# Differential attention in a two-layer diffusion backbone: values after two units in the program, three sets of turned halves, maps combined on VectorE, 16 of 18 key tiles turned by DMA

## The chip, the cores and the metric

The kernel runs on one core of a Trainium2 chip. Its time is the device time of one execution, in microseconds (us). Three executions of the kernel before took 4000.66, 4001.03 and 4004.86 us, so the median is 4001.03 us. In the text PE is TensorE, DVE is VectorE, ACT is ScalarE, POOL is GpSimd and SP is SyncE, whose queue issues all the DMAs spoken of here.

## The reference, cut to what matters

Two layers run over 2048 latent tokens and a prefix of 256 context tokens. The stage that the change touches is the differential attention of the second layer: four heads, each with two softmax maps over all 2304 keys, whose difference weighs the values.

```python
def diff_attend(q, k, v, lam):
    sc = jnp.einsum('bqhmd,bkhmd->bhmqk', q, k).astype(jnp.float32) * SCALE
    p = jax.nn.softmax(sc, axis=-1)
    a = (p[:, :, 0] - lam * p[:, :, 1]).astype(v.dtype)
    return jnp.einsum('bhqk,bkhe->bqhe', a, v)
```

Its output is normalised per head, gated, multiplied by the output projection, added to the residual stream and normalised once more. All of this runs in the same stage.

## The kernel before

The program is written with a tile framework: pools of buffers (a pool's `bufs` is how many copies of a tile exist), and a scheduler that orders the instructions of each engine by the written order, by priorities and by its own estimate of when each is ready. Each engine then works through its list strictly in that order. So an instruction that waits holds up everything behind it on its engine.

The stage starts at `c_pools` in `layer1` and covers the last 1240 us or so of the program. It works on 64 **units**: a unit is one head (of four) and one tile of 128 queries (of sixteen). Heads 0 and 1 come one after the other; heads 2 and 3 alternate in pairs of tiles. For each unit:

- `c_map` is called for map 1, then for map 0. PE multiplies the queries with the keys, which are kept as a high and a low half (`KH`, `KL`, float16). The scores go into two tiles in PSUM: `pSa` (1024 columns, 4 matmuls) and `pSb` (1280 columns, 6 matmuls). There is one copy of each, so the scores of the next map wait until the exponential has read those of this one. DVE takes the maxima (`mx`: one reduction over `pSa`, two over `pSb`), joins them (`cm`), makes the bias (`cnb`), and ACT writes the exponentials to `E1` or `E0` (two instructions, L1419), with their sums.
- From the sums DVE computes `rho`, the factor of map 1 against map 0.
- `c_halves` combines the two maps into `E1` (rho times map 1 plus map 0) and turns them so that keys lie on the partitions. Of the 18 key tiles, the first `DMAK` = 12 are combined on DVE in two instructions of 768 columns (L1432); the last 6 on POOL in two passes (L1429, L1430). The DMA part is cast to float16 on ACT (`H`), the remainder is subtracted on POOL (`L`), and `H` and `L` are each turned by two DMA transposes into `HT` and `LT`, issued from SP. The other 6 tiles are turned on PE into `pTr` (four, then two) and split into halves by ACT (`HT`) and DVE (`LT`).
- `c_values` multiplies the turned halves with the values: 3 matmuls for each of 18 key tiles, 54 in all, into `pO`. `finish` normalises and stores the result.

The loop in `layer1` writes the values one unit behind: the first half of the values of unit n-1 stands after map 1 of unit n, the second half after map 0, held in `pend`. `HT`, `LT`, `H`, `L` and `E1` have two copies, `E0` one. Between these steps `fill` lets a `Filler` put pieces of the output projection (`out_pair`: `yT`, `pX`, `ot`, `xo`) in at a fixed rate; `part` multiplies `ya` by the gate `gl` for it.

## Time and profile before

| | |
|---|---|
| median of three executions | 4001.03 us |
| the profiled execution's own time | 4010.3 us |
| its span in the profile | 4008.2 us |
| the stage, first `rho` to the end of the span | 2775.6 to 4008.2 us |
| PE, DVE, ACT, POOL busy over the whole span | 86%, 69%, 58%, 58% |

The page is one execution on the chip. Matmuls are pipelined, so PE counts as busy longer than it works; to see how fast PE works, take the distance between the starts of two matmuls, not the duration of one. A row of a timeline ends with the idle time of its engine before it and what ended that, in square brackets. The granted clock of TensorE has two levels in the rows, 1.00 (2.4 GHz) and 0.50 (1.2 GHz); a number between them is a mean over a stretch.

### The profile page before, as it was taken

Reading aid. Unit: us, or ns where it says so; the run is one execution under the profiler, and the core shown is the slowest. Engines: PE = TensorE matmul, PEld = TensorE weight load, DVE = VectorE, ACT = ScalarE, POOL = GpSimd, SP = SyncE. Lnnn points to the kernel's source line nnn. Section 1 sums busy time; section 2 is a strip of 40 time slices with the busy share of each in tenths; the row PEclk is TensorE's granted clock in tenths of the full one; section 3 lists DMA queues with packets and bytes.
Section 4 is the critical chain, followed back from the end, with each engine's and each line's share of the span. In section 5 each row is a group of like instructions: output and inputs, shape, how many; then the busy total and the mean of one; then the engine's idle time right before and its main releaser. Section 6 shows DMA issues by size and latency. Waiting matters only on the chain. (4 is left out here: it accounts for less than half of the span.)

```text
span 4008.2 us, 94016 instructions
## 1 busy us (share of the span) xinstructions
PE 3442.4 (86%) x37378; PEld 2679.9 (67%) x37378; DVE 2757.8 (69%) x6515; ACT 2334.3 (58%) x4294; POOL 2304.9 (58%) x2015
## 2 busy tenths in 40 slices
PE   7879989899989999999899999996677677677666
PEld 5659978789867777777688899984444444344443
DVE  5647788996576766665769986754666656666666
ACT  5215546556688877787636566664455444545554
POOL 3204466764388888887635553432565655666655
PEclk9989999999999999999999999998788888778888
DMA  7875433343521111110454442227344434233343
GB/s 235 209 188 121 109 79 97 82 100 89 151 88 47 57 47 47 48 58 27 152 118 94 99 117 73 67 78 206 90 98 117 98 86 116 63 91 96 88 91 83
DMA packets 657711, 400.69 MB, mean 100 GB/s; under 512 B 412342, under 2 KB 608246, under 8 KB 656758
## 3 DMA queue, kind: packets, MB, share of 16 engines
q1 hardware_dynamic: 657270, 394.68, 38.0%
q8 instruction: 292, 4.78, 0.5%
q14 instruction: 149, 1.22, 0.1%
HBM read 207.69 MB, written 106.90 MB: 78 GB/s over the span
## 5 line engine op out<-in xcount | busy, mean ns | idle before, releaser
L80 PE MATMUL pmm<-wk,hT 128*128 128x256 f16 x10848 | 1363.8, 276 | 63.1 <-DVE HL L365 18.8
L80 PEld LDWEIGHTS <-hT 128*128 128x128 f16 x10848 | 1035.4, 99 | 202.9 <-issue 47.5
L781 POOL TENSOR_TENSOR L<-Pm,H 128x1024 f16<-128x1024 f32 (+1 forms) x320 | 617.9, 1954 | 133.4 <-ACT H L779 82.9
L512 POOL TENSOR_TENSOR Pl<-Sb,Ph 128x640 f16<-128x640 f32 (+4 forms) x288 | 438.8, 1524 | 420.3 <-ACT Ph L511 253.2
L750 DVE TENSOR_REDUCE mx<-pM 128x1 f32<-128x512 f32 (+1 forms) x640 | 393.6, 634 | 218.8 <-PE pM L80 212.6
L80 PE MATMUL pO<-V,HT 128*128 128x128 f16 x2304 | 266.6, 239 | 196.4 <-DMA HT<-H 195.0
L80 PE MATMUL pX<-wo,yT 128*128 128x512 f16 x1554 | 400.9, 384 | 38.6 <-DVE yT L891 29.6
L776 ACT ACTIVATE Pm<-pS,esc_a 128x1024 f32<-128x1024 f32 (+1 forms) x320 | 324.5, 1027 | 150.6 <-PE pS L80 102.3
L80 PEld LDWEIGHTS <-Q 128*128 128x128 f16 x2072 | 218.0, 108 | 274.7 <-issue 191.1
L80 PEld LDWEIGHTS <-HT 128*128 128x128 f16 x2304 | 201.4, 108 | 239.2 <-DMA HT<-H 220.2
L80 PE MATMUL pO<-V,H 128*128 128x65 f16 (+1 forms) x4608 | 305.6, 193 | 1.4 <-DVE ya L1260 1.1
L779 ACT CAST H<-Pm 128x1024 f16<-128x1024 f32 (+1 forms) x320 | 302.2, 960 | 6.2 <-PE pO L80 0.3
L80 PEld LDWEIGHTS <-H 128*128 128x128 f16 x4608 | 264.9, 98 | 52.2 <-DVE ya L1260 2.8
L80 PEld LDWEIGHTS <-KL 65*128 65x128 f16 x2672 | 261.5, 98 | 52.2 <-issue 23.5
L80 PE MATMUL pO<-V,L 128*128 128x65 f16 x2304 | 277.4, 196 | 4.0 <-POOL L L781 3.6
L80 PE MATMUL pS<-Qt,KH 128*128 128x256 f16 x1152 | 279.5, 273 | 0.3 <-ACT Pm L776 0.3
L80 PE MATMUL pS<-Q,KL 65*128 65x256 f16 x1152 | 275.6, 274 | 0.0
L912 POOL TENSOR_TENSOR xo<-xo,ot 128x512 f32<-128x512 f32 x105 | 136.2, 1297 | 237.1 <-DVE ot L911 227.1
L80 PEld LDWEIGHTS <-yT 128*128 128x128 f16 x1632 | 155.1, 98 | 172.1 <-issue 36.9
L80 PE MATMUL pO<-V,LT 128*128 128x128 f16 x1152 | 238.4, 239 | 31.0 <-DMA LT<-L 20.5
L1419 ACT ACTIVATE E<-pSa,cnb,esc_c 128x1024 f32<-128x1024 f32 x128 | 154.0, 1203 | 160.5 <-DVE cnb L1415 155.1
L511 ACT CAST Ph<-Sb 128x640 f16<-128x640 f32 (+4 forms) x288 | 219.5, 762 | 47.9 <-PE pO L80 42.3
(327 smaller groups left out, 8569.4 us busy)
## 6 DMA issues: line engine op xcount, KB each, us to landing
qk<-qkst SPq DMA_DIRECT2D x104, 256.0 KB, 2.4
wmod<-w_mod SPq DMA_DIRECT2D x24, 1024.0 KB, 8.1
xo<-x SPq DMA_DIRECT2D x48, 512.0 KB, 3.8
xt<-x SPq DMA_DIRECT2D x34, 512.0 KB, 4.7
G<-zz SPq DMA_DIRECT2D x68, 256.0 KB, 2.4
x<-xo SPq DMA_DIRECT2D x34, 512.0 KB, 3.1
wst<-w_in_even SPq DMA_DIRECT2D x13, 1024.0 KB, 5.6
wst<-w_in_odd SPq DMA_DIRECT2D x13, 1024.0 KB, 5.7
```

The costliest lines, as they stand in the source:

```text
L80: return self.nc.tensor.matmul(out=out, lhsT=l, rhs=r, start=s, stop=e, skip_group_check=skip)
L511: nc.scalar.copy(out=H[:, :n * P], in_=Sb[:, :n * P])
L512: nc.gpsimd.tensor_tensor(out=L[:, :n * P], in0=Sb[:, :n * P], in1=H[:, :n * P], op=ALU.subtract)
L750: nc.vector.tensor_reduce(out=mx[:, j:j + 1], in_=ps[:, :n], op=ALU.max, axis=AX.X)
L776: nc.scalar.activation(out=Pm[:, :n], in_=S[:, :n], func=AF.Exp, scale=esc[0], bias=LNP)
L779: nc.scalar.copy(out=H[:, :n], in_=Pm[:, :n])
L781: eng.tensor_tensor(out=L[:, :n], in0=Pm[:, :n], in1=H[:, :n], op=ALU.subtract)
L912: (nc.vector if l and self.late else nc.gpsimd).tensor_tensor(out=xo[:, cs], in0=xo[:, cs], in1=tt, op=ALU.add)
L1419: nc.scalar.activation(out=E[:, c0:c0 + w], in_=S[i][:, :w], func=AF.Exp, scale=esc[0], bias=nb, accum_out=ss[:, i:i + 1])
```

## The change

All edits lie in the stage of differential attention.

- **Values two units behind.** `pend` becomes a list, and the loop writes the values of a unit only when two units are pending, so two steps after its maps; at the end the last two units' values follow one another. `HT` and `LT` get three copies.
- **Combining on DVE alone.** POOL's two passes are gone. DVE runs three instructions over columns 0 to 1024, 1024 to 2048 and 2048 to 2304.
- **16 of 18 key tiles turned by DMA.** `DMAK` is 16: `H`, `L` and each transpose are 1024 columns instead of 768, four transposes a unit as before. PE turns 2 tiles instead of 6.
- **Priority.** Both `c_map` calls of every unit are moved ahead by 80 in the scheduler's priority (`boostC`); before, only the first unit's map 1 was (by 1000).
- **Room.** The rotary tables get a pool of their own that is closed before the stage, and the gate tiles `gl` have one copy instead of two. The load of a head's values is written before the maps of its first unit, not after them.

```diff
-    DMAK = 12
+    DMAK = 16
+    boostC = 80
...
-        self.gp = self.pool(s, "gC", 2)
+        self.gp = self.pool(s, "gC", 1)
...
-        HT = self.wp.tile([P, NT, P], F16, name="HT")
-        LT = self.wp.tile([P, NT, P], F16, name="LT")
-        nc.gpsimd.tensor_scalar(out=E1[:, nd:], in0=E1[:, nd:], scalar1=rho, scalar2=None, op0=ALU.mult)
-        nc.gpsimd.tensor_tensor(out=E1[:, nd:], in0=E1[:, nd:], in1=E0[:, nd:], op=ALU.add)
-        for c0, c1 in ((0, nd // 2), (nd // 2, nd)):
+        HT = self.wp.tile([P, NT, P], F16, name="HT", bufs=3)
+        LT = self.wp.tile([P, NT, P], F16, name="LT", bufs=3)
+        for c0, c1 in ((0, nd // 2), (nd // 2, nd), (nd, NTOK)):
             nc.vector.scalar_tensor_tensor(out=E1[:, c0:c1], in0=E1[:, c0:c1], scalar=rho, in1=E0[:, c0:c1],
                                            op0=ALU.mult, op1=ALU.add)
...
+            self.rs.close()
             wo, kv = self.c_pools(s)
...
+            pend = []
+
+            def values(half):
+                if half == 0:
+                    self.Oc = self.pO.tile([P, 512], F32, name="pO")[:, 0:P]
+                u, halves, V, s0 = pend[0]
+                self.c_values(self.Oc, *halves, V, range(9) if half == 0 else range(9, NT))
+                if half:
+                    pend.pop(0)
+                    finish(u, self.Oc, s0)
...
-                with first:
+                with self.tc.high_priority(offset=self.early if n == 0 else self.boostC):
                     E1, s1 = self.c_map(u, 1, Qs[1, h, qt // 2][:, q], ks[1], escs[h // 2], shift[1])
-                if pend:
-                    O = self.pO.tile([P, 512], F32, name="pO")[:, 0:P]
-                    self.c_values(O, *pend[1], pend[2], range(0, 9))
+                if len(pend) == 2:
+                    values(0)
...
-                E0, s0 = self.c_map(u, 0, Qs[0, h, qt // 2][:, q], ks[0], escs[h // 2], shift[0])
+                with self.tc.high_priority(offset=self.boostC):
+                    E0, s0 = self.c_map(u, 0, Qs[0, h, qt // 2][:, q], ks[0], escs[h // 2], shift[0])
...
-                if pend:
-                    self.c_values(O, *pend[1], pend[2], range(9, NT))
-                    finish(pend[0], O, pend[3])
...
+                if len(pend) == 2:
+                    values(1)
+                pend.append((u, self.c_halves(E1, E0, rho), Vs[h], s0))
                 fill(n, 0.5)
```

Ahead of the stage the instructions of every engine stand in the same order as before, but for some independent ones that change places just before it. Inside it, three places show what moves. In the rows below a name's number tells one use of a buffer from another, and rows that only repeat are left out.

First, PE from the last scores of a unit's map 1 to the scores of its map 0. Before, the halves `HT_55408` belong to the unit before last, and `HT_55587` to the last unit, whose combined map is `E1_55473`:

```order
L80 MATMUL pSb_55629<-KL1_52319,Q1_54897 128x256
L80 LDWEIGHTS HT_55408
L80 MATMUL pO_55477<-V1_53194,HT_55408 128x128
L80 LDWEIGHTS LT_55409
L80 MATMUL pO_55477<-V1_53194,LT_55409 128x128
L80 LDWEIGHTS HT_55587
L80 MATMUL pO_55652<-V1_53194,HT_55587 128x128
L80 LDWEIGHTS Q0_54899
L80 MATMUL pSa_55699<-KH0_52322,Q0_54899 128x512
L1445 MATMUL pTr_55605<-idf_60,E1_55473 128x128 x4
```

Now, with `HT_55461` made from `E1_55344`, the combined map of the unit just before the scores `pSb_55502`:

```order
L80 MATMUL pSb_55502<-KH1_52156,Q1_54625 128x256
L80 MATMUL pSb_55502<-KL1_52159,Q1_54625 128x256
L1446 MATMUL pTr_55478<-idf_60,E1_55344 128x128 x2
L80 LDWEIGHTS HT_55461
L80 MATMUL pO_55694<-V1_52867,HT_55461 128x128
L80 LDWEIGHTS Q0_54627
L80 MATMUL pSa_55566<-KH0_52162,Q0_54627 128x512
L80 MATMUL pSa_55566<-KL0_52165,Q0_54627 128x512
L80 LDWEIGHTS LT_55462
L80 MATMUL pO_55694<-V1_52867,LT_55462 128x128
```

The turning of two tiles now stands directly behind map 1's scores, ahead of everything else; the first two values matmuls before map 0's scores belong to the unit just before, as they did before the change. Over the 63 such places, what PE has between map 1's scores and map 0's is on average 6.9 values matmuls, 1.1 turned tiles and 1.9 matmuls of the output projection before, and 5.6, 2.0 and 6.0 now; between `pSa` and `pSb` of map 0, 8.4 values matmuls and 1.6 turned tiles before, 13.1 and none now; behind map 0's scores, 37.8 values matmuls, 3.1 turned tiles and 7.9 of the projection before, 34.5, none and 4.7 now.

Second, DVE from `rho` of one unit to the bias `cnb1` of the next unit's map 1. Before:

```order
L1640 TENSOR_SCALAR rho_55723<-cs0_55720,cr1_55695 128x1
L1432 SCALAR_TENSOR_TENSOR E1_55648<-E1_55648,rho_55723,E0_55719 128x768 x2
L1411 TENSOR_REDUCE mx1_55815<-pSa_55813 128x1
L891 SCALAR_TENSOR_TENSOR yT_55795<-pX_55797,yT_55795 128x512
L1411 TENSOR_REDUCE mx1_55815<-pSb_55814 128x1 x2
L1413 TENSOR_SCALAR cm1_55829<-mx1_55815 128x1
L1415 TENSOR_SCALAR cnb1_55831<-cm1_55829,nesc_c0_50112 128x1
```

Now:

```order
L1652 TENSOR_SCALAR rho_55419<-cs0_55416,cr1_55391 128x1
L1414 TENSOR_REDUCE mx1_55503<-pSa_55501 128x1
L1433 SCALAR_TENSOR_TENSOR E1_55344<-E1_55344,rho_55419,E0_55415 128x1024 x2
L1433 SCALAR_TENSOR_TENSOR E1_55344<-E1_55344,rho_55419,E0_55415 128x256
L1414 TENSOR_REDUCE mx1_55503<-pSb_55502 128x1 x2
L1449 TENSOR_TENSOR LT_55462<-pTr_55478,HT_55461 128x256
L1416 TENSOR_SCALAR cm1_55517<-mx1_55503 128x1
L1418 TENSOR_SCALAR cnb1_55519<-cm1_55517,nesc_c0_50116 128x1
```

The third piece of the combination now stands ahead of `cnb1`, and here so does the split of the two turned tiles (`LT`). In 32 of 63 units the third piece stands behind the reductions over `pSb`, in 31 ahead of them. The reduction over `pSa` is done before `rho` in 48 of 63 units, where it was in 31.

Third, DVE from there to the bias `cnb0` of map 0. Before:

```order
L1411 TENSOR_REDUCE mx0_55880<-pSa_55878 128x1
L1635 TENSOR_SCALAR cr1_55874<-cs1_55834 128x1
L1636 RECIPROCAL cr1_55874<-cr1_55874 128x1
L1448 TENSOR_TENSOR LT_55766<-pTr_55783,HT_55765 128x512
L1411 TENSOR_REDUCE mx0_55880<-pSb_55879 128x1 x2
L911 SCALAR_TENSOR_TENSOR ot_55871<-pX_55806,am_55690,gate1_50468 128x512
L1413 TENSOR_SCALAR cm0_55894<-mx0_55880 128x1
L1415 TENSOR_SCALAR cnb0_55896<-cm0_55894,nesc_c0_50112,csh0_50094 128x1
```

Now:

```order
L1646 TENSOR_SCALAR cr1_55562<-cs1_55522 128x1
L1647 RECIPROCAL cr1_55562<-cr1_55562 128x1
L1414 TENSOR_REDUCE mx0_55568<-pSa_55566 128x1
L1414 TENSOR_REDUCE mx0_55568<-pSb_55567 128x1 x2
L1416 TENSOR_SCALAR cm0_55582<-mx0_55568 128x1
L1418 TENSOR_SCALAR cnb0_55584<-cm0_55582,nesc_c0_50116,csh0_50098 128x1
```

The split of four turned tiles (`LT`, 512 columns) is gone from between the reductions.

## Rows read from the trace of the kernel before

**Rows 1.** The page: span, and the clock granted in 40 slices.
```profile
span 4008.2 us, 94016 instructions
...
PEclk9989999999999999999999999998788888778888
```

**Rows 2.** Windows: length, each engine's busy time, granted clock, DMA share, GB/s.
```profile
2850.00:3900.00 1050.00, 732.72 (x5232) 448.85 (x5231) 668.69 (x1124) 533.58 (x968) 630.36 (x593) 0.84 0.40 94
...
3337.80:3344.50 6.70, 4.22 (x23) 2.96 (x24) 3.38 (x8) 3.90 (x7) 5.32 (x5) 0.50 0.56 113
...
3353.20:3357.60 4.40, 1.48 (x7) 0.48 (x5) 4.36 (x6) 1.18 (x2) 4.40 (x5) 1.00 0.89 187
```

**Rows 3.** Instructions by tile: shortest, median, longest ns; first and last start.
```profile
L1432 DVE SCALAR_TENSOR_TENSOR E<-E,rho,E x128: 1002/1020/2147, 2775.9 to 3969.7; 128x768 f32<-128x768 f32 x128
...
L1640 DVE TENSOR_SCALAR rho<-cs,cr x64: 262/267/275, 2775.6 to 3968.1; 128x1 f32<-128x1 f32 x64
```

**Rows 4.** Timeline of one unit: start, duration, engine, line, tiles, wait before.
```profile
3339.32 1.20 ACT L1419 ACTIVATE E<-pSa,cnb,esc_c 128x1024 f32<-128x1024 f32 x1 [1.19 <-DVE cnb L1415]
...
3340.01 0.39 PE L80 MATMUL pO<-V,HT 128*128 128x128 f16 x2 [4.77 <-DMA HT<-H]
...
3341.47 0.63 PE L80 MATMUL pSa<-KH,Q 128*128 128x512 f16 x1
...
3341.90 0.63 PE L80 MATMUL pSa<-KL,Q 128*128 128x512 f16 x1
...
3342.33 1.06 PE L1445 MATMUL pTr<-idf,E 128*128 128x128 f32 x4
...
3344.86 0.38 PE L80 MATMUL pSb<-KH,Q 128*128 128x512 f16 x1
...
3345.07 0.38 PE L80 MATMUL pSb<-KL,Q 128*128 128x512 f16 x1
...
3348.55 1.20 ACT L1419 ACTIVATE E<-pSa,cnb,esc_c 128x1024 f32<-128x1024 f32 x1 [1.82 <-DVE cnb L1415]
...
3351.35 0.27 DVE L1640 TENSOR_SCALAR rho<-cs,cr 128x1 f32<-128x1 f32 x1 [1.25 <-ACT E L1419]
...
3351.66 2.60 DVE L1432 SCALAR_TENSOR_TENSOR E<-E,rho,E 128x768 f32<-128x768 f32 x2
...
3351.79 2.97 POOL L1429 TENSOR_SCALAR E<-E,rho 128x768 f32<-128x768 f32 x1
...
3355.02 3.23 POOL L1438 TENSOR_TENSOR L<-E,H 128x768 f16<-128x768 f32 x2
...
3357.12 1.24 SPq L1440 DMA_TRANSPOSE LT<-L  x1
...
3358.04 1.20 ACT L1419 ACTIVATE E<-pSa,cnb,esc_c 128x1024 f32<-128x1024 f32 x1 [2.88 <-DVE cnb L1415]
```

**Rows 5.** Waits of PE from 2850 to 3900 us: total us, times, longest.
```profile
PE pO L80 <- DMA HT<-H: 174.7, 50, 7.5
...
PE pSa L80 <- ACT E L1419: 50.4, 47, 5.7
...
PE pO L80 <- DMA LT<-L: 19.8, 18, 2.9
...
PE pTr L1445 <- POOL E L1430: 17.8, 7, 5.2
```

**Rows 6.** Groups by form, 2850 to 3900 us: busy us, mean ns, idle before.
```profile
L80 PE MATMUL pSa<-KL,Q 128*128 128x512 f16 x224 | 109.1, 487 | 0.0
...
L80 PE MATMUL pSb<-KL,Q 128*128 128x512 f16 x224 | 98.2, 438 | 0.0
...
L1411 DVE TENSOR_REDUCE mx<-pSa 128x1 f32<-128x1024 f32 x112 | 136.7, 1220 | 85.4 <-PE pSa L80 82.0
...
L1411 DVE TENSOR_REDUCE mx<-pSb 128x1 f32<-128x768 f32 x112 | 105.7, 944 | 0.0
...
L1448 DVE TENSOR_TENSOR LT<-pTr,HT 128x512 f16<-128x512 f32 x56 | 38.4, 686 | 15.3 <-ACT HT L1447 15.2
```

More of the change, by code (lines that the diff above doesn't have):

```diff
@@ L1625, in layer1 @@
                     queries(n + 4)
[L1626 removed]
+                if qt == 0:
+                    Vs[h] = self.c_vals(h)
                 q = slice(qt % 2 * P, qt % 2 * P + P)
[L1628 removed]
+                with self.tc.high_priority(offset=self.early if n == 0 else self.boostC):
                     E1, s1 = self.c_map(u, 1, Qs[1, h, qt // 2][:, q], ks[1], escs[h // 2], shift[1])
[L1630 to L1632 removed]
+                if len(pend) == 2:
+                    values(0)
                 fill(n, 0.5)
@@ L1637, in layer1 @@
                 nc.gpsimd.tensor_scalar(out=r1, in0=r1, scalar1=nlam, scalar2=None, op0=ALU.mult)
-                E0, s0 = self.c_map(u, 0, Qs[0, h, qt // 2][:, q], ks[0], escs[h // 2], shift[0])
+                with self.tc.high_priority(offset=self.boostC):
+                    E0, s0 = self.c_map(u, 0, Qs[0, h, qt // 2][:, q], ks[0], escs[h // 2], shift[0])
                 rho = self.small("rho")
                 nc.vector.tensor_scalar(out=rho, in0=s0[:, 0:1], scalar1=s0[:, 1:2], scalar2=r1, op0=ALU.add, op1=ALU.mult)
-                if pend:
-                    self.c_values(O, *pend[1], pend[2], range(9, NT))
-                    finish(pend[0], O, pend[3])
-                if qt == 0:
-                    Vs[h] = self.c_vals(h)
-                halves = self.c_halves(E1, E0, rho)
-                fill(n, 0.5)
-                pend = (u, halves, Vs[h], s0)
-            O = self.pO.tile([P, 512], F32, name="pO")[:, 0:P]
-            self.c_values(O, *pend[1], pend[2], range(NT))
-            self.late = True
-            finish(pend[0], O, pend[3])
+                if len(pend) == 2:
+                    values(1)
+                pend.append((u, self.c_halves(E1, E0, rho), Vs[h], s0))
+                fill(n, 0.5)
+            while pend:
+                if len(pend) == 1:
+                    self.late = True
+                values(0)
+                values(1)
             filler.drain()
```

8 lines of the change are left out of this document (4 added, 4 removed).

## The prediction

> **What bounds the kernel now.** The page comes first: the clock of TensorE is granted at 0.9 or 1.0 until three quarters of the span, then at 0.7 and 0.8 [rows 1]. That last part is the stage that the change touches. The windows come second: from 2850 to 3900 us PE is busy for 733 of 1050 us, DVE for 669, POOL for 630, ACT for 534, and the DMA engines for 0.40 [rows 2]. No engine is full, so a chain through several engines sets the time. `rho` is made 64 times, first at 2775.6 and last at 3968.1 us [rows 3], which is 63 steps of 18.93 us. A step, times 63, is what has to be forecast.
>
> Third, the timeline of one unit, from the exponential of its map 1 at 3339.32 to that of the next unit at 3358.04, 18.72 us [rows 4]. It falls into two stretches. The first, 9.23 us, ends with the exponential of map 0 at 3348.55: `pSa` comes free at 3340.52 (3339.32 + 1.20), the scores of map 0 follow, 0.43 us from start to start (3341.47, 3341.90), then four turned tiles and values matmuls, then the scores in `pSb`, now 0.21 us from start to start (3344.86, 3345.07), the maxima and the bias. The second, 9.49 us, holds both exponentials of map 0, `rho` at 3351.35, the two combining instructions on DVE (2.60), the maxima of the next map 1 and its bias. In this second stretch PE has little to do: 1.48 us of the 4.40 from 3353.2 [rows 2]. One unit earlier the same idle place was a wait of 4.77 us [rows 4], and behind it the clock was granted at 0.50 from 3337.8 to 3344.5 [rows 2], just where map 0's scores run.
>
> Last, PE's waits: 174.7 us for `HT`, 50.4 for the exponential that frees `pSa`, 19.8 for `LT`, 17.8 for POOL's second pass [rows 5], over some 55 units (1050 / 18.93). The first looks like the prize, 3.1 us a unit. It mostly isn't: in the timeline the values that waited for `HT` start at 3340.01, and `pSa` came free only at 3340.52. PE would have stood until then anyway.
>
> **The change part by part**, in us a unit.
>
> *Values two behind.* In PE's list the first values matmuls before map 0's scores still belong to the unit just before; the scheduler has pulled them forward. The wait for `HT` keeps its place and its cover, the exponential. I count 0; what the third copy buys is that a late turn no longer blocks a buffer.
>
> *Third piece on DVE.* Reductions over 1024 and 768 columns take 1.220 and 0.944 [rows 6], 0.28 for 256 columns. A combining instruction of 768 takes 1.02 in the median [rows 3], so 1.30 for 1024 and 0.47 for 256: 1.30 + 1.30 + 0.47 = 3.07 where the unit shows 2.60. All of it lies between `rho` and `cnb1`, on the chain: **+0.47**. Ends: 0, where the next scores end later anyway; +1.1, since the longest was 2.15 instead of 1.02.
>
> *POOL's two passes.* 2.97 for the first in the unit, beside DVE [rows 4]. PE's turning waited 17.8 us for the second, 0.3 a unit, between the two score groups of map 0: **-0.3**, ends 0 and -0.6 (the wait and as much again behind it).
>
> *What PE has between the score groups of map 0.* Four tiles took 1.06 at half clock, 0.27 each; a values matmul has a quarter of the columns of a score matmul, 0.11. Gone are 1.6 tiles (0.43), come are 4.7 values matmuls (0.50): 0.
>
> *Longer halves.* Two subtractions on POOL took 3.23 [rows 4], 1.62 each, an estimated 2.15 for 1024 columns; a transpose held SP for 1.24, an estimated 1.65. Four of them make 6.6 of SP's 18, so the queue holds, and what stands behind them (`Q`, `y`, `ya`, `gl`) is loaded units ahead; the single `gl` waits for a product that is long done. But `LT` is wanted right behind the first score group of map 0. Its waits are 0.35 a unit now; without POOL's passes the subtraction starts sooner, with longer pieces it ends no sooner. I take **+0.4**, near today's row; ends -0.35 and +1.5, the latter if POOL's other work goes first.
>
> *Split on DVE.* 0.686 for 512 columns is gone from between the reductions of map 0 [rows 6]. It counts where the scores are already done: **-0.3**, ends 0 and -0.69. Beside it, behind map 0 PE has 3.3 values matmuls, 3.1 tiles and 3.2 projection matmuls less, at full clock 0.18 + 0.40 + 0.67, and the next scores start sooner: **-0.2**, as `rho` here waited for ACT and not for them; ends 0 and -0.9.
>
> *The new wait.* The two turned tiles wait for the third piece, and everything behind map 1's scores queues behind them: 5.6 values matmuls, 6.0 of the projection (1.9 before), map 0's scores. In the 32 units with the third piece behind the reductions it ends some 0.7 us before the exponential, so 1.9 before `pSa` is free; the queue then takes 0.3 + 0.3 + 1.3 = 1.9 at full clock, 3.7 at half. In the others there is a reduction pair more, and all fits. **+0.2**, ends 0 and +1.5.
>
> *Clock.* A score matmul's row is 0.38 at full clock and 0.63 at half [rows 4]. The means, both maps together, are 0.487 in `pSa` and 0.438 in `pSb` [rows 6], so if only map 0 meets the half clock, it does in 0.107 / 0.125 = 86% and 0.058 / 0.125 = 46% of cases. Each costs 0.215: four in `pSa` 0.74, the equal of five in `pSb` 0.50, and the values between them about 0.45: 1.7 a unit. PE's work no longer stops behind map 0's first scores, and the idle place is broken up by tiles and projection. I take half of it, **-0.8**; ends 0 and -1.7. Half, because the stretch from `rho` to `cnb1` still leaves PE little else.
>
> Sum: 0.47 - 0.3 + 0.4 - 0.3 - 0.2 + 0.2 - 0.8 = -0.53, times 63 = -33 us. The end of the program, 40 us behind the last `rho`, gets a second unit's values and loses POOL's passes: 0, give or take 8. The profiled execution took 4010.3 us against the median of 4001.0, so the span should fall from 4008 to about 3975, and the time to **3968 us**.
>
> **Rivals.**
>
> *The clock comes back wholly.* If the idle place is filled enough, all 1.7 is saved and the new wait costs nothing: 0.9 + 0.2 more, 69 us, **3899**. For it: PE's stretch behind `pSa` is now unbroken. Against: third piece and reductions leave the idle place its length.
>
> *The change does not do what it says.* The values keep their place in PE's list, the waits were cover, and the clock gives 0.3 instead of 0.8: 0.5 x 63 = 31 back, **3999**.
>
> *PE's queue behind the turned tiles (the other side).* Map 0's scores now stand behind a wait for DVE and up to twelve projection matmuls; if that comes at half clock in most units, the new wait costs 1.5 instead of 0.2: 82 us, **4050**. It decides from the point where what stands behind the tiles lasts longer than the 1.9 us until `pSa` is free.
>
> *POOL and DVE in each other's way.* The two combining instructions of the unit took 2.60 beside POOL's pass, against twice 1.02 [rows 3, 4]. The third piece meets POOL's first subtraction in 32 of 63 units. If it must wait for the rest of that, about 0.7, this costs 0.35 a unit, 22 us: **3990**. The Trainium skill (SBUF — State Buffer, "Who interferes with whom") says that a VectorE instruction with two SBUF inputs and a GpSimd instruction that reads SBUF exclude each other for a whole instruction. By that rule the second combining instruction could not have ended before POOL's pass did, at 3354.76; it ended at 3354.26, so the trace agrees only in part.
>
> **How the numbers follow.** The forecast gets 0.42 (its own range, 3935 to 3998, takes the clock between 0.3 and 1.3), the clock wholly back 0.18, no difference 0.13, PE's queue 0.20, POOL and DVE 0.07. A measurement of this kernel can tell about 0.2%, 8 us, from no change. Faster by more: 0.40 + 0.18 + 0.04 = 0.62. Within: 0.13 + 0.01 = 0.14. Slower: 0.20 + 0.04 for the ends of the others = 0.24. The range runs from the best case to PE's queue, **3893 to 4052**, since either alone has more than 0.1.
>
> **What would show it.** Combining: three DVE instructions of about 1.30, 1.30 and 0.47, POOL's L1429 and L1430 gone. Clock: the mean of the `pSa` score matmuls falls from 487 towards 430 ns and the granted mean rises over 0.84. `rho` steps of 18.4. The wait for `HT` on PE gives way to one of the turned tiles for DVE. I am wrong if the scores of map 0 start more than 1 us after `pSa` is free, if waits for `LT` grow over 1.5 us a unit, or if the clock stays at 0.84 and the steps still shrink.

## The result, and the profile after

The changed kernel took 4042.2 us in the median of four executions (4038.5 to 4045.0), the kernel before 4002.2 beside it: a ratio of 1.0099, with a 95% interval from 1.0081 to 1.0116. It is slower by 40 us where I had forecast 34 less. The time of the third rival (4050) came nearest.

First the page: span, and the granted clock in 40 slices, the stage of the change being the last quarter [rows 1].

```profile
span 4041.8 us, 93310 instructions
...
PEclk9989999999999999999999999997878887778888
```

The stretch from 2850 to 3900 us follows, and then two short ones (length, busy time of PE, its weight loads, DVE, ACT and POOL, granted clock, DMA share, GB/s). POOL's busy time fell from 630 to 434 us, the clock from 0.84 to 0.80 [rows 2].

```profile
2850.00:3900.00 1050.00, 702.25 (x4822) 407.65 (x4820) 652.46 (x1084) 508.43 (x879) 434.08 (x463) 0.80 0.46 106
...
3602.60:3607.50 4.90, 4.90 (x16) 2.17 (x17) 1.08 (x5) 2.96 (x5) 2.22 (x2) 0.59 0.84 161
3607.50:3610.00 2.50, 2.50 (x23) 1.53 (x21) 1.98 (x2) 0.27 (x1) 1.26 (x1) 1.00 0.00 0
```

By tile (shortest, median, longest ns; first and last start), the combination and `rho`. From the first `rho` to the last are 63 steps of 19.57 us, where it was 18.93 [rows 3]. That is 0.64 x 63 = 40 us, as much as the medians differ. The spans of the two profiled executions differ by less, 33.6 us: the first `rho` comes 4.0 us earlier, the end behind the last one is 2.6 us shorter, and the execution of the kernel before that was profiled took 8 us longer than its median.

```profile
L1433 DVE SCALAR_TENSOR_TENSOR E<-E,rho,E x192: 472/1279/2974, 2771.9 to 4007.4; 128x1024 f32<-128x1024 f32 x128, 128x256 f32<-128x256 f32 x64
L1652 DVE TENSOR_SCALAR rho<-cs,cr x64: 264/265/275, 2771.6 to 4004.3; 128x1 f32<-128x1 f32 x64
```

PE's waits in the same 1050 us (total, times, longest). The 174.7 for `HT` [rows 5] gave way to 211.3 for VectorE's third piece.

```profile
PE pTr L1446 <- DVE E L1433: 211.3, 54, 6.1
PE pSa L80 <- ACT E L1422: 63.0, 48, 3.5
PE pO L80 <- DMA HT<-H: 33.3, 20, 4.4
PE pO L80 <- DMA LT<-L: 17.9, 11, 3.0
```

Groups by form (busy us, mean ns, idle before). The score matmuls of `pSa` fell from 487 to 465 ns only [rows 6]; the third piece takes 770 ns where I had 470.

```profile
L80 PE MATMUL pX<-wo,yT 128*128 128x512 f16 x609 | 189.5, 468 | 6.6 <-ACT H L1438 5.7 <-DVE yT L893 0.9
...
L1433 DVE SCALAR_TENSOR_TENSOR E<-E,rho,E 128x1024 f32<-128x1024 f32 x108 | 141.0, 1346 | 1.5
...
L80 PE MATMUL pSa<-KL,Q 128*128 128x512 f16 x216 | 100.4, 465 | 0.0
...
L80 PE MATMUL pSb<-KL,Q 128*128 128x512 f16 x216 | 92.0, 426 | 0.0
...
L1433 DVE SCALAR_TENSOR_TENSOR E<-E,rho,E 128x256 f32<-128x256 f32 x54 | 41.6, 770 | 0.0
```

The first of these groups, the output projection, has a mean of 468 ns. Before, its row was

```profile
L80 PE MATMUL pX<-wo,yT 128*128 128x512 f16 x645 | 159.8, 387 | 28.7 <-DVE yT L891 26.9 <-DVE ot L911 1.2 <-DVE fss L926 0.5
```

Part of the half clock that left the scores fell on it: in units 5 to 60, 201 of these matmuls now start between map 1's exponential and map 0's scores, with a mean of 571 ns, where it was 23 before.

Last a timeline of the changed kernel, around the exponential of one unit's map 1 at 3603.07 (start, duration, engine, line; idle time before it in brackets).

```profile
3597.39 0.27 DVE L1652 TENSOR_SCALAR rho<-cs,cr 128x1 f32<-128x1 f32 x1
...
3597.56 0.27 PE L80 MATMUL pSb<-KL,Q 128*128 128x256 f16 x1
...
3597.70 2.48 DVE L1433 SCALAR_TENSOR_TENSOR E<-E,rho,E 128x1024 f32<-128x1024 f32 x2
...
3600.09 1.55 DVE L1414 TENSOR_REDUCE mx<-pSb 128x1 f32<-128x512 f32 x2
3600.14 4.38 POOL L1439 TENSOR_TENSOR L<-E,H 128x1024 f16<-128x1024 f32 x2 [2.09 <-ACT H L1438]
...
3601.56 0.98 DVE L1433 SCALAR_TENSOR_TENSOR E<-E,rho,E 128x256 f32<-128x256 f32 x1
3602.46 0.26 DVE L1416 TENSOR_SCALAR cm<-mx 128x1 f32<-128x1 f32 x1
3602.59 0.69 PE L1446 MATMUL pTr<-idf,E 128*128 128x128 f32 x2 [4.76 <-DVE E L1433]
3602.76 0.21 DVE L1418 TENSOR_SCALAR cnb<-cm,nesc_c 128x1 f32<-128x1 f32 x1
3603.07 1.20 ACT L1422 ACTIVATE E<-pSa,cnb,esc_c 128x1024 f32<-128x1024 f32 x1 [1.81 <-DVE cnb L1418]
3603.07 4.49 PE L80 MATMUL pX<-wo,yT 128*128 128x512 f16 x12
...
3607.51 0.38 PE L80 MATMUL pSa<-KH,Q 128*128 128x512 f16 x1
```

Map 1's scores are done at 3597.83 and PE stands for 4.76 us, until the third piece. Then twelve projection matmuls take 4.33 us (3603.07 to 3607.40), 0.36 each, in a stretch of 0.59 mean clock. `pSa` was free at 3604.27; map 0's scores start at 3607.51, 3.24 us later.

**Two stretches.** To compare the runs I cut each trace at the first exponential of each map and took means over units 5 to 60: the *first stretch* goes from map 1's exponential to map 0's, the *second* from there to the next unit's map 1. "Scores" is where the matmuls of map 0's scores begin and end, counted from map 1's exponential; "half" is the share of that time at 1.2 GHz, as a mean over the units. The step is (last `rho` - first) / 63. The two times in brackets hold a long tail and aren't compared.

| kernel | time, us | ratio to before, 95% | step | first | second | scores | half |
|---|---|---|---|---|---|---|---|
| before | 4002 | | 18.93 | 9.50 | 9.28 | 1.83 to 6.43 | 0.71 |
| changed | 4042 | 1.0081 to 1.0116 | 19.57 | 9.55 | 9.84 | 2.57 to 6.75 | 0.49 |
| x18 | 4051 | 1.0098 to 1.0128 | 19.74 | 9.80 | 9.77 | 2.71 to 7.15 | 0.79 |
| xpool | 4052 | 1.0103 to 1.0133 | 19.77 | 9.78 | 9.80 | 2.44 to 6.92 | 0.47 |
| xnoboost | 4034 | 1.0055 to 1.0086 | 19.41 | 9.67 | 9.53 | 2.26 to 6.72 | 0.42 |
| xone | 4061 | 1.0122 to 1.0156 | 19.83 | 9.53 | 10.14 | 2.50 to 6.94 | 0.56 |
| xlate2 | 4061 | 1.0132 to 1.0163 | 19.87 | 10.46 | 9.31 | 2.63 to 7.74 | 0.77 |
| xlate1 | 4023 | 1.0034 to 1.0070 | 19.10 | 8.68 | 10.22 | 2.13 to 6.20 | 0.35 |
| xlate0 | 3912 | 0.9755 to 0.9792 | 17.32 | 7.89 | 9.25 | 1.93 to 4.49 | 0.05 |
| xnowait | 4092 | 1.0208 to 1.0262 | 20.29 | 10.05 | 10.06 | 2.59 to 7.12 | 0.69 |
| xnothird | 4096 | 1.0215 to 1.0246 | 20.36 | 10.42 | 9.69 | 2.23 to 7.32 | 0.74 |
| xbtwo | 4027 | 1.0038 to 1.0072 | 19.14 | 9.72 | 9.27 | 2.12 to 6.60 | 0.59 |
| xb16 | 4085 | 1.0187 to 1.0217 | 20.14 | 10.13 | 9.87 | 1.91 to 7.43 | 0.54 |
| xbdve | 4122 | 1.0279 to 1.0310 | 20.83 | 10.97 | 9.69 | 4.42 to 8.27 | 0.26 |
| xnofillb | (4322) | | 18.20 | 9.60 | 8.57 | 1.37 to 6.92 | 0.73 |
| xnofilla | (4327) | | 18.18 | 9.09 | 9.07 | 1.41 to 6.54 | 0.78 |
| xwarm | 4148 | 1.0338 to 1.0371 | 21.17 | 10.19 | 10.73 | 3.51 to 7.26 | 0.29 |
| xl0one | 3919 | 0.9767 to 0.9800 | 17.38 | 7.79 | 9.44 | 1.92 to 4.49 | 0.07 |
| xplace | 4096 | 1.0207 to 1.0237 | 20.29 | 9.97 | 10.14 | 2.74 to 7.29 | 0.61 |
| xlatev | 3804 | 0.9479 to 0.9511 | 15.66 | 8.01 | 7.46 | 2.18 to 4.67 | 0.04 |

In all of these, `rho` starts 3.2 to 3.7 us behind map 0's exponential: 3.31 before, 3.53 in the changed kernel. So of the 0.56 that the second stretch grew, 0.22 lie ahead of `rho`: it starts 0.84 us behind ScalarE's last instruction on map 0 where it was 0.59, since VectorE is more often still at the reduction over the next `pSa`. The other 0.33 follow `rho`. There VectorE works with next to no gap, 0.13 us idle a unit before and 0.14 in the changed kernel. The durations of its instructions behind `rho`, which overlap a little, add up to 5.88 before and 6.31 now: the combination from 2.56 to 3.46, less 0.30 of `pSa` reductions that now run ahead of `rho`, less 0.22 of `yT`, and 0.09 more of the split.

### The profile page after: what moved, and what is told of

It reads as the page before. It is cut to its first block, busy times and chain, and to the rows that moved or that the text cites. A ratio compares the mean times of both kernels' runs of the same rounds, so it can differ in the third digit from the quotient of the medians.

```text
span 4041.8 us, 93310 instructions
## 1 busy us (share of the span) xinstructions
PE 3434.1 (85%) x37122; PEld 2649.9 (66%) x37122; DVE 2764.6 (68%) x6516; ACT 2324.7 (58%) x4230; POOL 2096.2 (52%) x1886
## 3 DMA queue, kind: packets, MB, share of 16 engines
q14 instruction: 148, 1.21, 0.1%
## 4 chain that ended last, share of the span: by engine, by line
PE 23%; DVE 13%; DMA 4%; issue 4%; ACT 3%; POOL 2%; SPq 1%; POOLq 0%; ACTq 0%; DVEq 0%
PE pmm L80 8%; PE pO L80 5%; DVE E L1433 4%; DVE mx L1414 3%; PE pX L80 3%; PE pSa L80 3%; ACT E L1422 2%; PE pSb L80 2%; PE pT L80 1%; DMA LT<-L 1%; DMA ya<-y 1%; DMA wst<-w_out_odd 1%; DMA HT<-H 1%; PE pS L80 1%; DVE wk L300 1%
## 5 line engine op out<-in xcount | busy, mean ns | idle before, releaser
L80 PE MATMUL pX<-wo,yT 128*128 128x512 f16 x1554 | 447.4, 422 | 13.4 <-ACT H L1438 7.1
L1439 POOL TENSOR_TENSOR L<-E,H 128x1024 f16<-128x1024 f32 x128 | 283.4, 2231 | 134.7 <-ACT H L1438 130.4
L80 PEld LDWEIGHTS <-yT 128*128 128x128 f16 x1632 | 169.4, 107 | 186.5 <-issue 66.3
L80 PE MATMUL pO<-V,HT 128*128 128x128 f16 x2304 | 255.0, 238 | 37.0 <-DMA HT<-H 36.7
L1414 DVE TENSOR_REDUCE mx<-pSa 128x1 f32<-128x1024 f32 x128 | 156.4, 1222 | 148.1 <-PE pSa L80 146.3
```

Of the source, the lines that this page charges most:

```text
L80: return self.nc.tensor.matmul(out=out, lhsT=l, rhs=r, start=s, stop=e, skip_group_check=skip)
L1414: nc.vector.tensor_reduce(out=mx[:, i:i + 1], in_=S[j][:, c:c + w], op=ALU.max, axis=AX.X)
L1439: nc.gpsimd.tensor_tensor(out=L, in0=E1[:, c0:c1], in1=H, op=ALU.subtract)
```

## Experiments

### Undoing one part of the change

All 18 tiles turned by DMA:

```diff
-    DMAK = 16
+    DMAK = 18
...
-        for c0, c1 in ((0, nd // 2), (nd // 2, nd), (nd, NTOK)):
+        for c0, c1 in ((0, nd // 2), (nd // 2, nd)):
```

> All 18 key tiles are turned by DMA, so nothing is turned on TensorE, and VectorE combines in two pieces of 1152 columns. Two theories of the loss of 0.64 us a unit (19.57 against 18.93). Queue theory: map 0's scores stand behind two turned tiles that wait 211 us (2850 to 3900 us) for VectorE's third piece; without them map 0's scores start again some 1.8 us behind the exponential of map 1 instead of 2.57, and the first stretch, 9.55 now, falls to about 9.0. Chain theory: what counts is that VectorE has a third piece (0.77) and the split of the turned tiles (0.42) between rho and the next map 1's bias; two pieces of 1152 cost about 2 x 1.5 = 3.0 instead of 3.46 and the split is gone, so the second stretch falls from 9.84 by 0.5 to 0.9, to about 9.1, and the first stays. Each alone gives about 4042 - 63 x 0.6 = 4005; both together about 3970. A rival, that longer transposes (1.24 us held SP for 768 columns, so 1.9 for 1152) make the low halves late, gives 4040 or more, with the wait for LT over 1 us a unit.

4051 us, above the changed kernel. The pieces cost 2.94 as expected and no tile is turned on PE, yet the first stretch is 0.25 longer than in the changed kernel and the second only 0.07 shorter: `HT` (269 us of PE's waits from 2850 to 3900) took the place of the tiles, and behind `rho` VectorE got `pSa` reductions (0.70 against 0.28) and `yT` (0.28 against 0.07) in place of what went. Both theories fall in this simple form. The rival's time came, but not its sign: the `LT` waits, 35 us over some 53 units, are 0.7 a unit.

The 256 columns combined on GpSimd, in two passes as before the change:

```diff
+        nc.gpsimd.tensor_scalar(out=E1[:, nd:], in0=E1[:, nd:], scalar1=rho, scalar2=None, op0=ALU.mult)
+        nc.gpsimd.tensor_tensor(out=E1[:, nd:], in0=E1[:, nd:], in1=E0[:, nd:], op=ALU.add)
-        for c0, c1 in ((0, nd // 2), (nd // 2, nd), (nd, NTOK)):
+        for c0, c1 in ((0, nd // 2), (nd // 2, nd)):
```

> Only the 256-column piece goes back to GpSimd, in two passes; VectorE keeps two pieces of 1024. Chain theory: the second stretch falls by the third piece, 0.5 to 0.8, to about 9.2, and the time to about 4042 - 63 x 0.6 = 4005. Queue theory: the turned tiles now wait for GpSimd's second pass, about 2 us behind rho, which is no later than the third piece ends now (3.5 behind rho); the wait shrinks, map 0's scores start earlier and the time falls too, by the first stretch. If neither falls (4042 within 8), what moved the time is not the third piece.

4052, so neither theory's fall came. The second stretch stayed at 9.80: with the piece gone, the split of the turned tiles (0.42, and 0.19 of waiting for them) stands ahead of the bias on VectorE in every unit.

No priority for the maps:

```diff
-    boostC = 80
+    boostC = 0
```

> The priority of the maps' scores is taken away and the rest stays. The tiles still stand directly behind map 1's scores in TensorE's order (2.0 of 2.0), with 3.5 values matmuls and 6.5 of the projection behind them instead of 5.6 and 6.0. Queue and chain theory: nothing changes, 4042 within 8. If the priority is what puts the tiles and the third piece where they hurt, the time returns to 4002.

4034, 8 us under the changed kernel (11 by the ratios), with intervals that just overlap. A fifth to a quarter of the loss, if it is real.

Values one unit behind:

```diff
-                if len(pend) == 2:
+                if pend:
```

> The values are written one unit behind again; the rest stays as changed. TensorE's order then holds 0.91 units pending at map 0's scores, as with two. Queue and chain theory: 4042 within 8, since the order hardly moves. If the depth itself costs (halves kept longer, queries and values colliding), the time falls by 20 or more; if the depth protects against late turns, as the third copy was meant to, it rises and the waits for HT come back towards 175 us.

4061: inside the changed kernel the second unit of depth is worth 19 us (16 by the ratios), as the last case of the expectation had it, but it is in the second stretch, and the `HT` waits rose to 61 us only.

### Moving VectorE's pieces past the next bias

All runs of this section start from the changed kernel. Here `c_halves` of a unit is called behind map 1 of the next one, and `issue_after` queues the pieces from index `first` on behind that map's bias on VectorE, and only there; the last unit has no next one.

```diff
+                if late:
+                    lu, lE1, lE0, lrho, lV, ls0 = late.pop()
+                    pend.append((lu, self.c_halves(lE1, lE0, lrho), lV, ls0))
...
-                pend.append((u, self.c_halves(E1, E0, rho), Vs[h], s0))
+                late.append((u, E1, E0, rho, Vs[h], s0))
...
+            with self.tc.issue_after(self.bias_ins.ins) if i >= first and not last else ExitStack():
                 nc.vector.scalar_tensor_tensor(out=E1[:, c0:c1], in0=E1[:, c0:c1], scalar=rho, in1=E0[:, c0:c1],
```

With `first` = 2 (the 256 columns moved):

> The combination of a unit is written behind map 1 of the next unit, and its third piece (256 columns) queues behind that map's bias; the first two stay between rho and the bias. Bias theory, formed from the runs so far: from rho to the next map 1's bias VectorE works without a gap (idle 0.14 us a unit in the changed kernel, 0.13 before), so a unit's time is what VectorE has there; taking 0.77 away (the mean of the third piece) gives 19.57 - 0.5 to 0.8 = 18.8 to 19.1 a unit, 3993 to 4010. Queue theory (TensorE's wait for the third piece, 211 us, sets the time): the third piece now ends later against map 0's scores, so the time rises, to 4050 or more.

The second stretch fell by 0.53, as the bias theory had it. The first rose by 0.91: map 0's scores run at half clock for 0.77 of their time, and take 5.11 us from first to last. What one stretch gives, the other can take back; no theory that looks at one of them alone is enough.

With `first` = 1:

> As the run with one piece moved, but two pieces (1024 and 256 columns) queue behind the next map 1's bias; one of 1024 stays ahead. Bias theory: another 1.35 (the mean of a piece) leaves the stretch, 17.5 to 17.9 a unit, 3915 to 3940, unless the scores of map 1 then end last: in the changed kernel they end 0.9 us behind rho's start in the mean, so a piece of 1.35 still covers them. Queue theory: 4050 or more.

4023. VectorE's busy time behind `rho` fell by 1.14, but it now waits there 1.49 us a unit, mostly for the scores of map 1. A miss of both numbers.

With `first` = 0:

> All three pieces queue behind the next map 1's bias. Bias theory: nothing but the reductions is left between rho and the bias; the scores of map 1 become the last thing, so little more than the run with one piece ahead, 16.5 to 17.8 a unit, 3850 to 3935, unless TensorE's order (13 values matmuls and 33 behind map 0 now stand ahead of the next scores) puts a wait for turned halves there. Queue theory: 4050 or more.

3912 us, 2.3% under the kernel before. TensorE's order now has 33 values matmuls between map 1's scores and map 0's where the changed kernel has 5.6; its longest idle place between the exponentials is 1.2 us in the mean (3.9 in the changed kernel), and map 0's scores hardly meet the half clock. Of the 2.25 us a unit that it gains on the changed kernel, 1.66 lie in the first stretch. The run moves VectorE's work and TensorE's order together and doesn't tell the two apart.

The third piece done, but not waited for:

```diff
-            nc.vector.scalar_tensor_tensor(out=E1[:, c0:c1], in0=E1[:, c0:c1], scalar=rho, in1=E0[:, c0:c1],
+            nc.vector.scalar_tensor_tensor(out=(E0 if c0 == nd else E1)[:, c0:c1], in0=E1[:, c0:c1], scalar=rho, in1=E0[:, c0:c1],
```

> VectorE's third piece writes into E0 instead of E1, so TensorE turns the last two tiles of map 1 uncombined and doesn't wait for the third piece (the output leaves out map 0 in the last 256 keys' columns); VectorE does the same work. Bias theory: the wait of 211 us goes and the time stays within 15 us of 4042. Queue theory: map 0's scores start at 1.8 instead of 2.57 us behind the exponential and the time falls by 0.5 a unit or more, below 4010.

4092. The wait of 211 us went, and one for `HT` of 243 us (in 1000) came; both stretches got longer. Map 0's scores start at 2.59, as late as in the changed kernel, so the large wait changed its name and not its place, and the queue theory falls. That the wait is cover isn't shown by this alone, since TensorE's order moved too: the two tiles now stand behind map 0's scores, and projection stands ahead of those in 24 of the 56 units instead of 38. The bias theory's 15 us are missed as well: `pSa` reductions (0.61 against 0.28) and `yT` (0.32 against 0.07) moved behind `rho`.

The third piece left out (TensorE turns the last two tiles as they are):

```diff
-        for c0, c1 in ((0, nd // 2), (nd // 2, nd), (nd, NTOK)):
+        for c0, c1 in ((0, nd // 2), (nd // 2, nd)):
```

> VectorE's third piece is left out altogether (the last 256 columns of map 1 go on uncombined, so map 0 is missing there). Against the run in which the third piece is done but not waited for (4092 us, stretches of 10.05 from the exponential of map 1 to that of map 0, and 10.06 from there to the next one of map 1), only VectorE's 0.77 is gone. Theory of the two stretches: the second one is VectorE's gap-free work and falls by 0.5 to 0.8, to 9.3 to 9.5; the first stays at about 10.0; 4041 to 4060. If VectorE isn't what sets the second stretch, the time stays within 15 us of 4092.

Against xnowait the second stretch fell by 0.37, less than expected, and the first rose by 0.37; the time is the same. Again VectorE's gain was handed back where map 0's scores run (0.74 at half clock, 5.1 us from first to last).

### One part alone, on the kernel before

Values two behind with three sets of halves, the loop and the room as in the change:

```diff
-        HT = self.wp.tile([P, NT, P], F16, name="HT")
-        LT = self.wp.tile([P, NT, P], F16, name="LT")
+        HT = self.wp.tile([P, NT, P], F16, name="HT", bufs=3)
+        LT = self.wp.tile([P, NT, P], F16, name="LT", bufs=3)
...
+                if len(pend) == 2:
+                    values(0)
```

> The kernel before with the values two behind and three sets of halves alone (12 tiles by DMA, the last six combined on GpSimd, no priority). VectorE's work between rho and the next bias is that of before, so theory of the two stretches: within 10 us of before. If depth is worth by itself what it was worth in the changed kernel (4061 with one behind, 4042 with two), the time falls by 15 to 20 us against before.

4027, 23 us over before. 0.21 a unit, all in the first stretch, and some 7 us at the end, where a second unit's values now stand.

16 tiles by DMA, the last two combined on GpSimd (with the room that the change makes):

```diff
-    DMAK = 12
+    DMAK = 16
```

> The kernel before with 16 of 18 tiles turned by DMA alone, the last two combined on GpSimd. VectorE's two pieces become 1024 columns, 2.7 instead of 2.56, and the split of two tiles comes ahead of the next bias (0.42) where that of six stood mostly behind it: the second stretch rises by 0.2 to 0.6; in TensorE's order the tiles and 4.6 projection matmuls stand ahead of map 0's scores as in the changed kernel. So 12 to 50 us over before. If these were free, no difference.

4085, 81 over before, more than expected: the tiles stand ahead of map 0's scores and 19.8 values between its two groups, where before had 8.4. The scores end at 7.43.

The combination on VectorE alone, with six tiles on PE:

```diff
-        nc.gpsimd.tensor_scalar(out=E1[:, nd:], in0=E1[:, nd:], scalar1=rho, scalar2=None, op0=ALU.mult)
-        nc.gpsimd.tensor_tensor(out=E1[:, nd:], in0=E1[:, nd:], in1=E0[:, nd:], op=ALU.add)
-        for c0, c1 in ((0, nd // 2), (nd // 2, nd)):
+        for c0, c1 in ((0, nd // 2), (nd // 2, nd), (nd, NTOK)):
```

> The kernel before with the combination on VectorE alone: three pieces of 768 columns, no pass on GpSimd. Theory of the two stretches: a third piece of 1.02 to 1.3 enters VectorE's gap-free work, and 5.8 tiles that wait for it and 22 values matmuls stand ahead of map 0's scores in TensorE's order: second stretch 10.2 to 10.6, first no shorter, 60 to 120 us over before. If GpSimd's passes had been worth what I gave them (0.3 a unit), the rise is 20 us less; if VectorE has room, no rise.

4122, 119 over before. Of PE's waits from 2850 to 3850 us the first row is

```profile
PE pTr L1443 <- DVE E L1430: 127.6, 48, 5.5
```

and map 0's scores begin at 4.42. The time is within the expectation and its place is not: the second stretch is 9.69 where I had 10.2 to 10.6, and the first grew by 1.47. This is the rival of PE's queue in full: 5.8 tiles that wait for the third piece, and 22 values behind them. The three parts alone cost 23 + 81 + 119 us, together 40: they are not terms of one sum.

### The projection and the clock

No piece of the projection between the units (all of it runs behind the last), in the changed kernel and in the one before:

```diff
-    rateC = (5.3, 5.4)
+    rateC = (0.0, 0.0)
```

> The changed kernel with no piece of the output projection put between the units; all of it runs behind the last unit, so the time as a whole is long and only the step from rho to rho counts. Projection theory: the step falls to that of the units which today have no projection ahead of map 0's scores, 18.2 to 18.6 us (19.57 with it). VectorE theory: the step falls only by the projection's own instructions on VectorE beside the path, about 0.3, to about 19.2.

> The kernel before with no piece of the output projection between the units; only the step counts. Its units without projection ahead of map 0's scores take 18.75, those with it 18.82, so 18.5 to 18.8. Projection theory: the changed kernel's step is then shorter than this one by 0.2 to 0.5, as I forecast for the whole. VectorE theory: it is longer by 0.4 to 0.6, as with the projection.

By tile, the combination and `rho` of the changed kernel without projection, then of the one before without it:

```profile
L1433 DVE SCALAR_TENSOR_TENSOR E<-E,rho,E x192: 475/1279/1287, 2765.5 to 3913.0; 128x1024 f32<-128x1024 f32 x128, 128x256 f32<-128x256 f32 x64
L1652 DVE TENSOR_SCALAR rho<-cs,cr x64: 261/265/273, 2764.8 to 3910.3; 128x1 f32<-128x1 f32 x64
```

```profile
L1432 DVE SCALAR_TENSOR_TENSOR E<-E,rho,E x128: 1006/1156/1661, 2764.2 to 3911.2; 128x768 f32<-128x768 f32 x128
L1640 DVE TENSOR_SCALAR rho<-cs,cr x64: 261/265/274, 2763.4 to 3909.9; 128x1 f32<-128x1 f32 x64
```

18.18 against 18.20 us a step: on the maps alone the change does nothing. The two stretches cancel, 0.51 less in the first stretch and 0.50 more in the second. This is the cleanest pair of the study, since TensorE's order is the same in nearly every unit. The loss of 0.64 appears only with the projection, which costs 0.73 a unit in the kernel before (18.93 - 18.20) and 1.39 in the changed one. Neither theory had said that both steps would be equal; the projection theory is right on the place, and overrated what is left without it.

Empty matmuls in PE's idle place:

```diff
+        if m == 1:
+            for _ in range(28):
+                self.mm(S[1][:, 1280:1536], Q, KH[:, 0:256], True, True)
```

> The changed kernel with 28 empty matmuls of 256 columns behind map 1's scores of every unit (they write columns of pSb that nobody reads), where TensorE waits for the turned tiles today. Clock theory: the half clock at map 0's scores (0.49 of their time now) goes to under 0.2, the span of these scores falls from 4.19 to about 3.1 us, what stands ahead of them runs at full clock, and the time falls by 0.8 to 1.4 a unit, to 3955 to 3990, though TensorE does 3 us more a unit. If the clock costs nothing on the path, 4042 or, with the empty work in the way, more.

This one prices nothing. The half clock at map 0's scores did fall, to 0.29, but the empty matmuls write the tile that the reductions over `pSb` read, and those of map 1 now waited 0.75 us a unit where they waited for nothing in the changed kernel. That is about half of the 1.60 that a step grew; map 0's scores also start 0.94 later. The row by form, from 2850 to 3850 us, has the idle time ahead of the reductions of both maps, of which map 0's had 58 us in the changed kernel too:

```profile
L1417 DVE TENSOR_REDUCE mx<-pSb 128x1 f32<-128x512 f32 x96 | 66.2, 689 | 83.5 <-PE pSb L80 83.2
```

The projection's pieces written in one place, behind map 0's maps:

```diff
-                fill(n, 0.5)
                 r1 = self.small("cr1")
...
+                fill(n, 1.0)
                 rho = self.small("rho")
...
-                fill(n, 0.5)
```

> The changed kernel with the projection's pieces written in one place, right behind map 0's maps, at the same rate. TensorE's order then has projection ahead of map 0's scores in 24 units instead of 39. Projection theory: each such unit costs 1.49 us more (19.87 against 18.38 in the changed kernel), so 15 x 1.49 = 22 us less, about 4020. If the projection costs the same wherever it stands, 4042 within 8.

4096. Projection stands ahead of map 0's scores in 24 units instead of 39, and the time rose by 54 us. Units without it there take 19.87 us in this run, those with it 20.44: the 1.49 between the two kinds of unit in the changed kernel is not a price that goes wherever the matmuls go. VectorE got 0.63 more behind `rho` (the `pSa` reductions and `yT` came back there), while `rho` itself came 0.26 sooner; 8.5 values now stand ahead of map 0's scores, which start at 2.74 where it was 2.57 and take 0.37 longer.

### A version that beats both

The late combination (`first` = 0) with values one unit behind:

```diff
-                if len(pend) == 2:
+                if pend:
```

> The run with all three pieces behind the next map 1's bias (3912 us), with the values written one unit behind instead of two. TensorE's order holds 1.01 units pending at map 0's scores against 1.02, so if the order decides, 3912 within 10. If the third set of halves and the second pending unit are what makes the late combination possible, 3940 or more.

3919 against 3912, with overlapping intervals: the late combination doesn't need the depth.

The late combination, with all values behind map 1's last scores on TensorE:

```diff
                 if len(pend) == 2:
-                    values(0)
+                    with self.tc.issue_after(self.last_score.ins):
+                        values(0)
+                        values(1)
...
-                if len(pend) == 2:
-                    values(1)
```

> The run with all three pieces behind the next map 1's bias (3912 us, steps of 17.32), with one more edit: all values matmuls queue behind map 1's last scores, so map 1's ten score matmuls follow one another, 54 values come behind them, and map 0's ten follow one another too. There the scores of map 1 end 14.24 us behind the exponential with up to 24 values among them at half clock, and VectorE waits 1.50 a unit for them. If that wait is on the path it goes, 1.0 to 1.5 a unit: 3818 to 3850. If the 54 values now make map 0's scores late instead (they have some 2.7 us until pSa is free and need 3 to 6.5), no gain: 3912 within 15.

3804 us, 5.1% under the kernel before, and better than expected. The wait that the expectation named went: from `rho` to the next exponential it is 4.13 us in the mean where xlate0 has 5.71, and VectorE's idle time in it fell from 2.17 to 0.70. From 2850 to 3750 us (columns as above), the windows of xlate0 and of this one:

```profile
2850.00:3750.00 900.00, 645.26 (x4654) 388.08 (x4651) 626.59 (x1043) 476.77 (x853) 420.74 (x447) 0.86 0.52 117
```

```profile
2850.00:3750.00 900.00, 676.69 (x5178) 410.65 (x5178) 672.33 (x1163) 529.75 (x948) 440.45 (x497) 0.90 0.58 130
```

One unit of it on VectorE, from `rho` to the next bias and on to the pieces, 4.38 us from the start of `rho` to the end of the bias where the unit above took 5.58:

```profile
3306.56 0.27 DVE L1658 TENSOR_SCALAR rho<-cs,cr 128x1 f32<-128x1 f32 x1 [2.84 <-ACT E L1422]
3306.75 1.22 DVE L1414 TENSOR_REDUCE mx<-pSa 128x1 f32<-128x1024 f32 x1
3308.83 1.56 DVE L1414 TENSOR_REDUCE mx<-pSb 128x1 f32<-128x512 f32 x2 [0.87 <-PE pSb L80]
3310.42 0.27 DVE L1416 TENSOR_SCALAR cm<-mx 128x1 f32<-128x1 f32 x1
3310.73 0.21 DVE L1418 TENSOR_SCALAR cnb<-cm,nesc_c 128x1 f32<-128x1 f32 x1
3310.86 2.87 DVE L1434 SCALAR_TENSOR_TENSOR E<-E,rho,E 128x1024 f32<-128x1024 f32 x3
```

## Why the prediction was wrong

The views were read rightly: no engine is full, the step decides, and 63 times its growth is the loss. The largest wait, called cover before the change, went for the most part (174.7 to 33.3 us) and map 0's scores start no sooner; in xnowait its successor went as well, and the time did not fall. The sum failed at these terms, the first two above all.

- **Clock, -0.8: nothing.** The argument was that PE's idle place would be broken up. The longest idle place between the exponentials grew instead, from 3.4 to 3.9 us in the mean, since everything behind the turned tiles queues for the third piece. Without projection it did shrink, from 4.24 to 3.10, and the half clock at map 0's scores went from 0.73 to 0.78 all the same. With projection it went from 0.71 to 0.49, that is from 3.39 to 2.42 us a unit; but between map 1's exponential and these scores, where the projection now stands, it rose from 1.37 to 2.08, and behind them, for the most part in the idle place, from 1.21 to 3.17. The signs that I had named, `pSa` matmuls near 430 ns and a granted mean over 0.84, read 465 and 0.80.
- **The new wait, +0.2: 0.74.** Map 0's scores start that much later than before. I had put a mean of six projection matmuls behind the tiles, at full clock, and found that all fits. In the changed kernel 18 of 56 units have none there and start 1.67 us behind the exponential; the other 38 start at 2.99, and in the unit shown it was twelve, most of the time at half clock (0.59). A mean over unlike units hid the case in which the scores come late. The rival had its mechanism and place right, and the stated sign (over 1 us behind `pSa`, here 2.57 - 1.20 = 1.37) came. Without projection the start moved by 0.04.
- **What PE has between the score groups, 0: -0.4.** From first to last map 0's scores take 0.42 less without projection, as 3.9 tiles are gone from between them and the values there stay at 17.5. With projection they take 0.41 less, but there their half clock fell too, and the two causes aren't separated.
- **Split, POOL's passes, `LT`: -0.3, -0.3, +0.4.** From the end of map 0's reductions to its exponential it is 1.35 us before and 1.19 after: -0.16 for the split (-0.27 from the end of the scores). The wait for POOL's pass went, but the turned tiles wait longer in another place. `LT` waits are 0.33 a unit (17.9 / 54) where they were 0.36, so nothing.
- **A shorter list behind map 0, -0.2: the sooner start came, the gain didn't.** The next map 1's scores start 1.55 us behind map 0's exponential where it was 1.99, and end 0.52 sooner. But from `rho` on VectorE had 0.13 us of idle time a unit to give. What ran sooner was the reduction over `pSa`, and `rho` came 0.22 later behind it.
- **Third piece, +0.47: right alone, larger in company.** Without projection the second stretch grew by 0.50, which holds the split of the turned tiles too (0.24 a unit, where none stood there), so the fit is in part luck. With it, the pieces cost 3.46 where I had 3.07, for the reason below, and the second stretch grew by 0.56, 0.22 of it ahead of `rho`.
- **Values two behind, 0:** 23 us dearer alone and 16 to 19 us cheaper within the change. The end of the program was within its bounds (-3 of 0 plus or minus 8).
- **The priority** had no term of its own; it costs 8 to 11 us, if that is real. **The room** (one copy of `gl`, the values loaded earlier) was taken to be free, and no run has it alone.

Put together: on the maps alone the first stretch gained 0.51 where I had -1.0 for it, the second lost 0.50 where I had 0.47, which is no difference; and the projection, which had no term of its own, made the change 0.66 dearer, 0.56 of it in the first stretch. With it the first stretch grew by 0.05: 0.74 for the start of the scores, -0.41 for their span, -0.27 behind them.

How the 0.66 divides between the order on TensorE, its clock and VectorE stays open: xplace moved all three at once. The two kinds of unit in the changed kernel give a hint, though they differ in more than the projection. With projection ahead, map 0's scores start 1.32 later, but take 1.05 less (3.85 against 4.90), 1.62 us of it at half clock against 4.10. From their end to the exponential it is 0.48 more, where VectorE has `yT` (0.30) and `xo` (0.27), and from `rho` to the next exponential 0.76 more, where it has 0.42 of `pSa` reductions. So in these units most of what the queue costs comes back, and most of the 1.49 stands beside VectorE's work.

## What to carry to other kernels

Cut a unit at the events that the chain can't do without and read each piece apart; a term that shortens one piece may be paid back in the next, by the clock or by what moves there, so price an idle place of TensorE by what runs right behind it. Before adding work to an engine that already works without a gap between two links of the chain, ask whether any of it can stand behind the next link: the whole combination behind the next bias, with the order on TensorE that came of it, was worth 91 us against the kernel before (with one piece of three moved the kernel was 58 slower than that), and an unbroken order on TensorE 108 more. Background work that is laid in at a fixed rate needs a term of its own, counted for the units that it meets, not as a mean over all.

## What the runs showed of the hardware

In the changed kernel a combining piece of 256 columns takes 0.48 us in 35 of 64 units: in 6 with nothing on POOL, in 6 beside a short POOL instruction, in 23 begun ahead of POOL's subtraction. In the other 29 it begins inside a POOL instruction, 28 times a subtraction, and takes 0.98 (24 times) to 2.34; each of the 28 ends 0.28 us behind the end of that subtraction. In the timeline above it starts inside the first of POOL's two subtractions (3600.14, 4.38 for both) and takes 0.98, while the reductions over PSUM ahead of it take their usual 1.55 beside the same pass. In another unit it was the last of three pieces that had begun ahead of POOL:

```profile
3122.02 2.88 DVE L1433 SCALAR_TENSOR_TENSOR E<-E,rho,E 128x1024 f32<-128x1024 f32 x3
```

```profile
3124.46 2.42 POOL L1439 TENSOR_TENSOR L<-E,H 128x1024 f16<-128x1024 f32 x1 [3.48 <-ACT H L1438]
```

There the three took 2.88 (1.28 + 1.28 + 0.48, with starts that overlap a little), and the subtraction took 2.42 where its shortest was 2.11. Who comes second waits. The Trainium skill (SBUF — State Buffer, "Who interferes with whom") says that the shared port pair is an exclusive lock, that whoever issues first has it for the whole instruction, and that reductions never contend. Here the trace agrees on the first two but for 0.2 us, since a piece of 0.48 ends 0.28 behind the subtraction that it waited for, and on the third for these reductions, which read PSUM. In the prediction I had given this rival 0.35 a unit; the third piece's 0.77 against 0.47 is 0.30.
